# Attention scores in a hybrid encoder layer: 64 queries of two heads over 320 keys, and the softmax division moved to the output stage

## The chip, the cores and the metric

The kernel runs on one core of one Trainium2 chip. The metric is device microseconds (us) of one execution. Five engines work side by side, each through its own instructions in order: TensorE (PE in the profile, its weight loads PEld), VectorE (DVE), ScalarE (ACT), GpSimd (POOL) and SyncE (SP), which only issues transfers. They wait for one another through semaphores.

## The reference

One layer over 4096 positions of width 1024: RMS norm, one input projection, two groups of heads side by side, one output projection, residual, and a last RMS norm. Group A is a bidirectional mLSTM (4 heads of 128), group B windowed attention. The change touches group B:

```python
scores = jnp.einsum('bnqhgd,bnkhd->bnhgqk', qb, kw) * (B_HEAD_DIM ** -0.5)   # 8 query heads, 2 kv heads, 64 wide
...
mask = (jnp.abs(rel) <= WINDOW)[None, :, :] & key_ok[:, None, :]             # WINDOW = 128, BLOCK = 128
scores = jnp.where(mask[None, :, None, None], scores + bias, NEG_INF)
sink_l = sink.astype(jnp.float32).reshape(B_KV_HEADS, Q_PER_KV)[:, :, None]
m = jnp.maximum(jnp.max(scores, axis=-1), sink_l)
p = jnp.exp(scores - m[..., None])
denom = jnp.sum(p, axis=-1) + jnp.exp(sink_l - m)
out = jnp.einsum('bnhgqk,bnkhd->bnqhgd', p, vw) / denom.transpose(0, 1, 4, 2, 3)[..., None]
...
y_b = windowed_gqa(qh, kh, vh, sink, rel_bias) * jax.nn.silu(z_b.astype(jnp.float32))
y = jnp.concatenate([y_a, y_b], axis=-1).astype(x.dtype)
return x + y @ w_out.astype(x.dtype)
```

A block of 128 queries sees three blocks of 128 keys, but each query only the 257 keys within 128 of it; 64 neighbouring queries together see 64 + 256 = 320 keys.

## The kernel before, in words

All work is in float32, most products split into a high and a low part (tiles of type fp32r), so that a product is two or three matmuls. Four passes follow one another: `pass1` (norm and transposes of x, the q, k and v projections of group B and all its attention, the gates of group A, and the first values of group A), `pass2` (group A's q, k, v and its backward states), `pass3` (group A's scan, its gates, the first part of group B's gate) and `tail` (the rest of group B's gate in `zunits`, then the output projection with a Strassen scheme, two row blocks a pair, class `OutPair`).

Attention goes in 64 slots; slot `sl` is query block `n = sl // 2` and key head `kv = sl % 2`, with four query heads. In `att_a(sl, g)` head g's scores are made by two matmuls (high and low part of k) of up to 384 columns into the PSUM tile `sp`; one DVE instruction (line 280) adds the bias, writes the tile `s` in SBUF and takes the row maximum. After the fourth head: the maximum against the sink (line 286), four exponentials on ACT that also sum (line 288), the sink's own term (290, 291), the sum and its reciprocal (292, 293), and four multiplications on POOL by that reciprocal (line 295). `att_t` transposes the four heads' tiles in pieces of 128 keys on PE (line 307), `att_o` multiplies them by v (line 321), and ACT and DVE add the two halves of the result into `ab` (lines 332, 333), which goes to DRAM as `at_d`.

On PE the order is the one in which the Python code is written (`manual_schedule`): `interleave` spreads the attention pieces of `slot` between projection matmuls. On the other engines a scheduler sets the order by priority and by its own estimate of when inputs are there. Each engine then runs its list strictly in order. At the end of pass 1 the hooks `w2_load` (splitting the weights of group A's projections, lines 478 to 483) and `gate1`, `gate2`, `gate3` run between the last slots; `gp` (line 595) needs `G`, the end of a chain of DVE instructions on 128x256 (lines 566 to 577).

Keys sit in tiles `kk` of 512 columns, the first 256 copied from the tile before (line 391, DVE). The pool `w8` has 12 buffers of 8 KB a partition for weights, `kk` and bias; the pool `x4` has 14 buffers of 4 KB, which in the output stage hold a pair's two input tiles `y` and its seven operands `yo`.

In the output stage each pair is seven products of 12 matmuls; `prep(i)` makes operand i of the next pair (sums on DVE, a high part on ACT, a low part on DVE, line 1195), `evict` adds the products into the rows (line 1220), `finish` norms and stores them.

Of the kernel before, what the change touches and what calls it, by code (L numbers as in the profile page):

```python
# [36 lines left out]
def setup(nc, tc, A, es):  # L37
# [126 lines left out]
def pass1(c):  # L164
    nc, tc, A = c.nc, c.tc, c.A
    NB = 16
    with ExitStack() as es:
# [56 lines left out]
        def small_loads():  # L224
            r = {}
            r["oh"] = xtile(c, [33, 512], F32, "oh")
            nc.sync.dma_start(r["oh"], A["onehot"])
            r["rb"] = wk.tile([33, 8], F32, name="rb")
            nc.gpsimd.memset(r["rb"][32:33, :], 1.0)
            nc.sync.dma_start(r["rb"][0:32, :], A["rel_bias"])  # L230
            r["gb"] = c.cp.tile([128, 2, 2, 4], F32, name="gb")
            nc.sync.dma_start(r["gb"], A["gate_b"].partition_broadcast(128).rearrange("p (a b d) -> p a b d", a=2, b=2))
            sink = r["sink"] = c.cp.tile([128, 8], F32, name="sink")
            nc.sync.dma_start(sink, A["sink"].partition_broadcast(128))
            r["nsink"] = c.cp.tile([128, 8], F32, name="nsink")
            nc.vector.tensor_scalar(r["nsink"], sink, -1.0, None, ALU.mult)
            return [r[k] for k in ("oh", "rb", "gb", "sink", "nsink")]
# [10 lines left out]
        def bias_gather():  # L248
            bias.extend(c.wp.tile([128, 4, 384], F32, tag="w8", name=f"bias{j}") for j in range(2))
            flat = c.bv_d.rearrange("h q r -> (h q r)")  # L250
            for t in range(2):
                for a in range(4):
                    src = bass.AP(tensor=flat.tensor, offset=flat.offset + t * 4 * 32 * 512 + 127 - 32 * a,
                                  ap=[[511, 32], [32 * 512, 4], [1, 384]])
                    nc.sync.dma_start(bias[t][32 * a:32 * a + 32, :, :], src)

        KK, Q, V, XT, ST = {}, {}, {}, {}, {}

        def att_a(sl, g):
# [6 lines left out]
            qb, qc = Q[n // 2], (n % 2) * 128  # L266
            hs = slice(kv * 4, kv * 4 + 4)
            if g == 0:
# [3 lines left out]
            mx, ng, rs, sk, rd = [st[:, i, :] for i in range(5)]  # L272
            h = kv * 4 + g
            sp = c.ps("a", [128, 384], f"sp{n}_{h}")
            qt = qb[h // 2][:, h % 2, qc:qc + 128]
            for z in range(2):
                nc.tensor.matmul(sp[:, jl:jr], qt, kk[:, kv, z, col - 128 + jl:col - 128 + jr],  # L277
                                 start=(z == 0), stop=(z == 1))
            s = wk.tile([128, 384], F32, tag="s", bufs=13, name=f"s{n}_{h}")
            nc.vector.tensor_tensor_reduce(out=s[:, jl:jr], in0=sp[:, jl:jr], in1=bias[kv][:, g, jl:jr],  # L280
                                           op0=ALU.add, op1=ALU.max, scale=1.0, scalar=-3e38,
                                           accum_out=mx[:, g:g + 1])
            ps.append(s)
            if g < 3:
                return
            nc.vector.scalar_tensor_tensor(ng, mx, -1.0, nsink[:, hs], ALU.mult, ALU.min)  # L286
            for g in range(4):
                nc.scalar.activation(ps[g][:, jl:jr], ps[g][:, jl:jr], AF.Exp, bias=ng[:, g:g + 1],  # L288
                                     accum_out=rs[:, g:g + 1])
            nc.vector.tensor_add(sk, sink[:, hs], ng)  # L290
            nc.scalar.activation(sk, sk, AF.Exp)
            nc.vector.tensor_add(rd, rs, sk)
            nc.vector.reciprocal(rd, rd)
            for g in range(4):
                nc.gpsimd.tensor_tensor(out=ps[g][:, jl:jr], in0=ps[g][:, jl:jr],  # L295
                                        in1=rd[:, g:g + 1].broadcast_to([128, jr - jl]), op=ALU.mult)

# [14 lines left out]
        def att_o(sl, i):  # L312
# [16 lines left out]
            o = slice(64, 128) if kv == 0 else slice(0, 64)  # L329
            ov = op.rearrange("p (g q) -> p g q", g=4)  # L330
            with tc.high_priority(offset=EV):
                nc.scalar.copy(ab[a], ov[o])
                nc.vector.tensor_add(ab[a], ov[a], ab[a])  # L333
            if kv:
# [41 lines left out]
        def kproj(b):  # L376
            R = {}

            def unit(k, j):
# [10 lines left out]
                if b > 0:  # L390
                    nc.vector.tensor_copy(kk[:, :, :, 0:256], f32(KK[b - 1][:, :, :, 256:512]))
                with tc.high_priority(offset=EV):
# [46 lines left out]
        def qproj(b):  # L439
# [3 lines left out]
            def unit(m, k, j):  # L443
# [7 lines left out]
                if k < KT - 1 or j < 2:  # L451
                    return
                qt = wk.tile([128, 2, 256], F32R, tag="q", bufs=6, name=f"q{b}_{m}")
                with tc.high_priority(offset=EV):
                    for z in range(2):
                        a = slice(z * 64, z * 64 + 64)
                        o = slice(64 - z * 64, 128 - z * 64)
                        nc.scalar.activation(qt[a, z, :], qp[a, :], AF.Copy, scale=0.125)
                    for z in range(2):
                        a = slice(z * 64, z * 64 + 64)  # L460
                        o = slice(64 - z * 64, 128 - z * 64)
                        nc.vector.scalar_tensor_tensor(qt[o, z, :], qp[a, :], 0.125, f32(qt[a, z, :]),
                                                       ALU.mult, ALU.subtract)
# [147 lines left out]
def gate3(c, wk):  # L611
# [20 lines left out]
    nc.gpsimd.memset(one, 1.0)  # L632
    c.g = cl, cm, a, b, ml, dec, one


# [68 lines left out]
def pass2(c):  # L704
    nc, tc, A = c.nc, c.tc, c.A
    with ExitStack() as es:
# [137 lines left out]
        for b in range(7, -1, -1):  # L844
# [306 lines left out]
class OutPair:  # L1151
    def __init__(self, c, wk, j):
# [3 lines left out]
        for i in range(2):  # L1156
            n = 2 * j + i
            y = xtile(c, [128, KT, 128], F32, f"y{n}")
            nc.sync.dma_start(y, c.y_d[n])
            self.y.append(y)  # L1160
        if j == NCH // 2 - 1:
            for i in range(2):
# [100 lines left out]
def tail(c):  # L1263
    nc, tc, A = c.nc, c.tc, c.A
    c.psum({"pj": 8})
    with ExitStack() as es:
# [13 lines left out]
        for b in range(1, 8):  # L1280
# [55 lines left out]
        for j in range(NCH // 2):  # L1336
# [3 lines left out]
            for i in (0, 1, 2, 3, 5, 4, 6) if end else range(7):  # L1340
                p.product(i, None if end or i == 0 else (lambda i=i: nxt.prep(i - 1)))
                if i in ((2, 3) if end else (3, 5)) and j:
                    finish(2 * j - (1 if i == (3 if end else 5) else 2), p.dve)
# [31 lines left out]
def host(x, norm_w, w_in, conv_w, conv_b, gate_b, mhn_w, sink, rel_bias, w_out, final_norm_w):  # L1375
# [18 lines left out]
        "conv_b": a(a(conv_b)[0].reshape(8, 128).T),  # L1394
        "gate_b": a(gate_b)[0], "mhn": a(a(mhn_w)[0].reshape(4, 128).T), "sink": a(sink)[0],
        "rel_bias": a(rel_bias), "w_out": a(a(w_out)[0][rp]), "fnw": a(final_norm_w), "onehot": onehot,
# [17 lines left out]
```

## Time and profile before

| | |
|---|---|
| median of 3 runs | 2251.96 us (2250.21 to 2254.26) |
| the profiled execution | 2251.49 us, of which the span from first to last instruction is 2249.8 us |
| mean granted clock of TensorE | 0.996 |
| PE | 2200.6 us busy, 98% of the span |
| PEld | 1912.0 us, 85% |
| DVE | 1464.8 us, 65% |
| ACT | 1094.3 us, 49% |
| POOL | 628.8 us, 28% |
| bytes moved | 376.08 MB |

By place in the span: pass 1 to about 646 us, pass 2 to 1230 us, pass 3 and the gate to 1930 us, the output stage to the end. A group row of the profile has the line, engine, operation, tiles and shapes, the count, then busy time and mean ns of one, then the engine's idle time just before and what ended it. Matmuls overlap one another, so the mean ns of one is longer than the distance from one to the next; the latter is read from start times.

### The profile page before, as it was taken

To read this page: it belongs to the slowest core of one execution; us is meant where nothing else is said; L and a number is where in the kernel's file an instruction comes from. 1 tells how busy PE (TensorE), PEld (TensorE's weight loads), DVE (VectorE), ACT (ScalarE), POOL (GpSimd) and SP (SyncE) were. 2 spreads that over 40 slices of the span, in tenths; PEclk is the share of its full clock that TensorE was granted. 3 is DMA by queue.
4 is the path that set the end of the run, shared out by engine and by line. 5 is a ranking of instruction groups with operands and counts; after the bars stand their busy time and mean duration, and the time that the engine had idled before them with its cause. 6 is when DMAs were issued, how large, how long until landed. Compare 5 with 4: busy or idle time off the path is not lost.

```text
span 2249.8 us, 36150 instructions
## 1 busy us (share of the span) xinstructions
PE 2200.6 (98%) x12432; PEld 1912.0 (85%) x12432; DVE 1464.8 (65%) x3253; ACT 1094.3 (49%) x2710; POOL 628.8 (28%) x978
## 2 busy tenths in 40 slices
PE   6999999999989999999999999999999999999998
PEld 6999999999888888888888788888888888888887
DVE  5888888888966655665568555555554452766776
ACT  5777877787743433443346444444443231333332
POOL 2545454544623112211122111112111111112222
PEclk9999999999999999999999999999999999999999
DMA  8332323231224414442464877667776799466664
GB/s 236 124 106 93 121 78 127 76 123 57 94 76 152 142 62 148 160 141 70 138 208 154 290 245 237 225 211 246 237 229 191 274 364 307 143 166 169 169 170 129
DMA packets 257803, 376.08 MB, mean 167 GB/s; under 512 B 19507, under 2 KB 151219, under 8 KB 257620
## 3 DMA queue, kind: packets, MB, share of 16 engines
q1 hardware_dynamic: 238452, 307.90, 42.6%
q0 software_dynamic: 19024, 65.68, 9.7%
q8 instruction: 98, 1.61, 0.3%
q14 instruction: 85, 0.70, 0.1%
q10 hardware_dynamic: 144, 0.20, 0.0%
HBM read 253.18 MB, written 120.52 MB: 166 GB/s over the span
## 4 chain that ended last, share of the span: by engine, by line
PE 89%; DMA 4%; DVE 3%; ACT 2%; issue 1%; SPq 0%; POOL 0%; POOLq 0%; DVEq 0%; ACTq 0%
PE up L759 15%; PE o L1206 14%; PE zp L1050 7%; PE op L1050 7%; PE qp L449 7%; PE v2p L732 7%; PE op L321 4%; PE sp L277 4%; PE tp L307 3%; PE zbp L154 3%; PE zbp L156 3%; PE zbp L155 3%; PE num L1003 2%; PE num L1002 2%; PE kp L385 2%; PE vp L417 2%
## 5 line engine op out<-in xcount | busy, mean ns | idle before, releaser
L759 PE MATMUL up<-xb,w 128*128 128x512 f32 x1344 | 338.6, 396 | 0.0
L1206 PE MATMUL o<-wo,yo 128*128 128x512 f32 (+1 forms) x1356 | 312.1, 392 | 0.0
L1206 PEld LDWEIGHTS o<-wo,yo 128*128 128x128 f32 x1356 | 253.1, 188 | 59.1
L759 PEld LDWEIGHTS up<-xb,w 128*128 128x128 f32 x1344 | 243.9, 189 | 47.2
L295 POOL TENSOR_TENSOR s<-s,st 128x384 f32<-128x384 f32 (+1 forms) x256 | 205.2, 833 | 233.2 <-ACT pt L309 83.2
L777 DVE SCALAR_TENSOR_TENSOR qk<-U,cw,qk 128x512 f32<-128x512 f32 x256 | 190.2, 755 | 92.6 <-ACT qk L775 87.9
L449 PE MATMUL qp<-xT,wqb 128*128 128x256 f32 x1536 | 246.6, 289 | 0.2 <-DVE xT L362 0.2
L449 PEld LDWEIGHTS qp<-xT,wqb 128*128 128x128 f32 x1536 | 220.1, 191 | 9.5 <-issue 1.1
L1050 PE MATMUL op<-w,xs 128*128 128x512 f32 x720 | 202.4, 408 | 1.1 <-DMA xs<-xT_d 1.1
L1050 PE MATMUL zp<-w,xs 128*128 128x512 f32 x720 | 187.8, 401 | 1.8 <-DVE z L1059 1.8
L288 ACT ACTIVATE s<-s,st 128x384 f32<-128x384 f32 (+1 forms) x256 | 153.1, 600 | 28.6 <-DVE st L286 27.9
L732 PE MATMUL v2p<-w,xb 128*128 128x512 f32 x672 | 157.6, 394 | 0.8 <-DMA xb<-xT_d 0.8
L280 DVE CUSTOM_DVE_ANT_0 s<-sp,bias 128x384 f32<-128x384 f32 (+1 forms) x256 | 138.6, 542 | 27.3 <-PE sp L277 16.1
L1050 PEld LDWEIGHTS zp<-w,xs 128*128 128x128 f32 x720 | 130.7, 188 | 28.9 <-DVE z L1059 2.3
L732 PEld LDWEIGHTS v2p<-w,xb 128*128 128x128 f32 x672 | 126.0, 188 | 31.1 <-DMA xb<-xT_d 1.7
L1017 ACT ACTIVATE hs<-num,r 128x128 f32<-128x128 f32 x128 | 46.9, 368 | 215.8 <-DVE r L1014 168.5
L1050 PEld LDWEIGHTS op<-w,xs 128*128 128x128 f32 x720 | 126.5, 189 | 22.8 <-ACT hs L1017 1.5
L277 PE MATMUL sp<-kk,q 128*128 128x384 f32 (+1 forms) x512 | 134.6, 344 | 3.1 <-DVE st L280 3.1
L310 DVE TENSOR_TENSOR pt<-tp,pt 128x512 fp32r<-128x512 f32 x188 | 128.5, 684 | 13.7 <-ACT pt L309 9.8
L309 ACT CAST pt<-tp 128x512 fp32r<-128x512 f32 x188 | 109.9, 585 | 55.6 <-PE tp L307 53.1
L321 PE MATMUL op<-pt,v 128*128 128x512 f32 x376 | 121.8, 405 | 7.9 <-DVE ab L333 7.8
L307 PE MATMUL tp<-ident,s 128*128 128x128 f32 x752 | 112.8, 272 | 0.0
(259 smaller groups left out, 4456.3 us busy)
## 6 DMA issues: line engine op xcount, KB each, us to landing
xT_d<-xT SPq DMA_DIRECT2D x128, 256.0 KB, 2.3
xc<-xT_d SPq DMA_DIRECT2D x64, 512.0 KB, 8.2
xs<-xT_d SPq DMA_DIRECT2D x120, 256.0 KB, 6.5
xb<-xT_d SPq DMA_DIRECT2D x48, 514.0 KB, 9.2
x<-x SPq DMA_DIRECT2D x32, 512.0 KB, 4.8
E<-m_d SPq DMA_DIRECT2D x64, 256.0 KB, 4.8
W<-w_d SPq DMA_DIRECT2D x64, 256.0 KB, 5.9
y<-y_d SPq DMA_DIRECT2D x32, 512.0 KB, 4.1
```

Of the source, the lines that this page charges most:

```text
L277: nc.tensor.matmul(sp[:, jl:jr], qt, kk[:, kv, z, col - 128 + jl:col - 128 + jr], start=(z == 0), stop=(z == 1))
L280: nc.vector.tensor_tensor_reduce(out=s[:, jl:jr], in0=sp[:, jl:jr], in1=bias[kv][:, g, jl:jr], op0=ALU.add, op1=ALU.max, scale=1.0, scalar ...
L288: nc.scalar.activation(ps[g][:, jl:jr], ps[g][:, jl:jr], AF.Exp, bias=ng[:, g:g + 1], accum_out=rs[:, g:g + 1])
L295: nc.gpsimd.tensor_tensor(out=ps[g][:, jl:jr], in0=ps[g][:, jl:jr], in1=rd[:, g:g + 1].broadcast_to([128, jr - jl]), op=ALU.mult)
L307: nc.tensor.transpose(tp[:, g * 128:(g + 1) * 128], ps[g][:, j * 128:(j + 1) * 128], c.ident)
L321: nc.tensor.matmul(op, vt, pt[:, z, :], start=(i == 0 and z == 0), stop=(i == len(js) - 1 and z == 1))
L449: nc.tensor.matmul(qp, wq[k // 2][:, k % 2, w, m * 128:m * 128 + 128], x[k], start=(k == 0 and j == 0), stop=(k == KT - 1 and j == 2))
L732: nc.tensor.matmul(vp, a, wv[k // 2][:, k % 2, m, :], start=(k == 0 and j == 0), stop=(k == KT - 1 and j == 2))
L759: nc.tensor.matmul(up[:, 0:hi - lo], w[k // 2][:, k % 2, a, cs], x, start=(k == 0 and j == 0), stop=(k == KT - 1 and j == 2))
L777: nc.vector.scalar_tensor_tensor(acc, U[:, t:t + 512], cw[:, cm, t:t + 1], acc, ALU.mult, ALU.add)
L1050: nc.tensor.matmul(P[nm], XS[n](a, k), w[:, m, :], start=(k == 0 and j == 0), stop=(k == KT - 1 and j == 2))
L1206: nc.tensor.matmul(p, a[:, z, k, :], w[k // 2][:, k % 2, m, lo:hi], start=k == 0 and z == 1, stop=k == 3 and z == 0 and m == 0)
```

## The change

Scores: instead of one head's 128 queries over 384 keys, a piece `g` is now one half `h = g // 2` of the query block (64 queries) of two heads together (again 128 rows), over the 320 keys from 64h on. So q is stored as [4 groups of 64 queries, 2 heads, 64], the bias table is one tile [128, 4, 320] instead of two of [128, 4, 384], and the sink is loaded in the new row order. The tiles `s` become 12 fixed ones (`SB`), whose 64 columns outside the 320 are set to zero once, by POOL at the start; transposes and products with v stay as they were. In `att_o` only the column order changes.

Division: the reciprocals are kept in a tile `R`, and POOL's four multiplications are gone. After `gate4` in pass 2, `rnorm` transposes `R` on PE and stores it as `r_d`. In the output stage each `OutPair` loads the two blocks' reciprocals, each row copied to 64 partitions (tile `rb`, four transfers), and `scale` multiplies the attention half of both `y` tiles by it on DVE, before `prep(1)`.

Keys: the copy of 256 columns of `kk` goes from DVE to POOL.

```diff
+    c.r_d = dp.tile([NCH, 2, 4, 128], F32, name="r_d")
+    c.R = c.cp.tile([128, NCH, 2, 4], F32, name="R")
...
-            bias.extend(c.wp.tile([128, 4, 384], F32, tag="w8", name=f"bias{j}") for j in range(2))
+            bias.append(c.wp.tile([128, 4, 320], F32, tag="w8", name="bias"))
...
+        SB = [[wk.tile([128, 384], F32, name=f"s{h}_{i}") for i in range(6)] for h in range(2)]
+        for t in SB[0]:
+            nc.gpsimd.memset(t[:, 320:384], 0.0)
+        for t in SB[1]:
+            nc.gpsimd.memset(t[:, 0:64], 0.0)
...
+            half, m = g // 2, g % 2
+            lo, hi = max(jl, 64 * half), min(jr, 320 + 64 * half)
...
-            qt = qb[h // 2][:, h % 2, qc:qc + 128]
+            qt = qb[kv * 2 + m][:, qc // 64 + half].rearrange("p z q -> p (z q)")
             for z in range(2):
-                nc.tensor.matmul(sp[:, jl:jr], qt, kk[:, kv, z, col - 128 + jl:col - 128 + jr],
+                nc.tensor.matmul(sp[:, lo:hi], qt, kk[:, kv, z, col - 128 + lo:col - 128 + hi],
                                  start=(z == 0), stop=(z == 1))
-            s = wk.tile([128, 384], F32, tag="s", bufs=13, name=f"s{n}_{h}")
+            s = SB[half][(2 * sl + m) % 6]
...
-            nc.vector.reciprocal(rd, rd)
-            for g in range(4):
-                nc.gpsimd.tensor_tensor(out=ps[g][:, jl:jr], in0=ps[g][:, jl:jr],
-                                        in1=rd[:, g:g + 1].broadcast_to([128, jr - jl]), op=ALU.mult)
+            nc.vector.reciprocal(c.R[:, n, kv, :], rd)
...
-                    nc.vector.tensor_copy(kk[:, :, :, 0:256], f32(KK[b - 1][:, :, :, 256:512]))
+                    nc.gpsimd.tensor_copy(kk[:, :, :, 0:256], f32(KK[b - 1][:, :, :, 256:512]))
...
-                        nc.scalar.activation(qt[a, z, :], qp[a, :], AF.Copy, scale=0.125)
+                        nc.scalar.activation(qt[a, :, z, :], qv[a], AF.Copy, scale=0.125)
...
+def rnorm(c):
+    nc = c.nc
+    tp = c.ps("b", [128, 2, 128], "rtp")
+    for i in range(2):
+        nc.tensor.transpose(tp[:, i, :], c.R[:, 16 * i:16 * i + 16].rearrange("p n a g -> p (n a g)"), c.ident)
+    rt = xtile(c, [128, 2, 128], F32, "rt")
+    nc.scalar.copy(rt, tp)
+    for i in range(2):
+        nc.sync.dma_start(c.r_d[16 * i:16 * i + 16].rearrange("n a g q -> (n a g) q"), rt[:, i, :])
...
                 if b == 7 and m == 6:
                     gate4(c)
+                    rnorm(c)
...
+        self.rb = rb = xtile(c, [128, 2, 2, 4, 64], F32, f"rb{j}")
+        for i in range(2):
+            for a in range(2):
+                src = c.r_d[2 * j + i, a].rearrange("g q -> (g q)")
+                nc.sync.dma_start(rb[64 * a:64 * a + 64, i].rearrange("p h g q -> p (h g q)"), src.partition_broadcast(64))
...
+    def scale(self):
+        for i in range(2):
+            b = self.y[i][:, 4:8].rearrange("p g (h q) -> p h g q", h=2)
+            self.c.nc.vector.tensor_mul(b, b, self.rb[:, i])
...
                 p.product(i, None if end or i == 0 else (lambda i=i: nxt.prep(i - 1)))
+                if i == 0 and not end:
+                    nxt.scale()
```

PE's list is the same row by row except for the 192 or 320 columns of the `sp` matmuls and the two transposes of `R`. Three places on the other engines follow.

POOL at the end of pass 1, where `w2s` and `w2_..` are pieces of group A's weights and `s29_0` is head 0's tile of query block 29. Before:

```order
L295 TENSOR_TENSOR s29_0_8158<-s29_0_8158,st58_8154 128x384
L295 TENSOR_TENSOR s29_1_8174<-s29_1_8174,st58_8154 128x384
L295 TENSOR_TENSOR s29_2_8200<-s29_2_8200,st58_8154 128x384
L295 TENSOR_TENSOR s29_3_8235<-s29_3_8235,st58_8154 128x384
L478 TENSOR_TENSOR w2s10_8827<-w2s10_8827,nw_86 128x512
L480 TENSOR_TENSOR w2_10_8826<-w2s10_8827,w2_10_8826 128x512
L495 MEMSET v2t31_8453 128x8
```

and now, around the same weight pieces:

```order
L492 TENSOR_TENSOR w2_04_7679<-w2s04_7680,w2_04_7679 128x512
L490 TENSOR_TENSOR w2s10_8337<-w2s10_8337,nw_87 128x512
L492 TENSOR_TENSOR w2_10_8336<-w2s10_8337,w2_10_8336 128x512
L507 MEMSET v2t31_7992 128x8
L490 TENSOR_TENSOR w2s14_8356<-w2s14_8356,nw_87 128x512
L492 TENSOR_TENSOR w2_14_8355<-w2s14_8356,w2_14_8355 128x512
```

The multiplications between the weight pieces are gone.

DVE at the end of pass 1, around the instruction that completes `G` (line 577 before, 589 now). Before:

```order
L310 TENSOR_TENSOR pt61_1_8740<-tp61_1_8735,pt61_1_8740 128x512
L293 RECIPROCAL st62_8604<-st62_8604 128x4
L333 TENSOR_TENSOR ab30_8747<-op60_8698,ab30_8747 64x512
L575 SCALAR_TENSOR_TENSOR g0_8581<-g0_8581 128x256
L280 ISA s31_7_8755,st63_8690<-sp31_7_8752,bias1_326 128x256
L280 ISA st63_8690 128x1
L483 SCALAR_TENSOR_TENSOR w2_22_8946<-w2s22_8947,nw_86,w2_22_8946 128x512
L483 SCALAR_TENSOR_TENSOR w2_22_8946<-w2s23_8951,nw_86,w2_22_8946 128x512
L577 SCALAR_TENSOR_TENSOR G_89<-g0_8581 128x256
```

and now:

```order
L306 RECIPROCAL R_91<-st62_8130 128x4
L320 TENSOR_TENSOR pt61_0_8236<-tp61_0_8231,pt61_0_8236 128x512
L587 SCALAR_TENSOR_TENSOR g0_8107<-g0_8107 128x256
L320 TENSOR_TENSOR pt61_1_8255<-tp61_1_8250,pt61_1_8255 128x512
L589 SCALAR_TENSOR_TENSOR G_90<-g0_8107 128x256
L292 ISA s1_1_156,st63_8208<-sp63_3_8267,bias_352 128x192
L292 ISA st63_8208 128x1
L344 TENSOR_TENSOR ab30_8262<-op60_8215,ab30_8262 64x2x4x64
```

`G` is now completed ahead of the last scores, the addition into `ab30` and the two weight pieces.

DVE in the output stage, while pair 4's products run; `y12`, `y13` are the inputs of pair 6, `xr8` the rows of pair 4. Before:

```order
L1220 TENSOR_TENSOR xr8_21117<-o2_4_0_21150,xr8_21117 128x512
L1183 TENSOR_TENSOR s6_1_21306<-y13_21196 128x512
L1195 TENSOR_TENSOR yo5_5_21251<-s5_4_21223,yo5_5_21251 128x512
L1195 TENSOR_TENSOR yo5_6_21261<-y11_21047,yo5_6_21261 128x512
L1184 TENSOR_TENSOR s6_1_21306<-s6_1_21306,y12_21194 128x512
```

and now:

```order
L1254 TENSOR_TENSOR xr8_20674<-o2_4_0_20709,xr8_20674 128x512
L1229 TENSOR_TENSOR yo5_5_20815<-s5_4_20787,yo5_5_20815 128x512
L1207 TENSOR_TENSOR y12_20753<-y12_20753,rb6_20757 128x2x4x64
L1207 TENSOR_TENSOR y13_20755<-y13_20755,rb6_20757 128x2x4x64
L1254 TENSOR_TENSOR xr8_20674<-o3_4_0_20729,u4_20673 128x512
```

The two multiplications by `rb6` stand ahead of the eviction of pair 4's product 3.

More of the change, by code (lines that the diff above doesn't have):

```diff
@@ L232, in small_loads @@
             nc.sync.dma_start(r["gb"], A["gate_b"].partition_broadcast(128).rearrange("p (a b d) -> p a b d", a=2, b=2))
-            sink = r["sink"] = c.cp.tile([128, 8], F32, name="sink")
-            nc.sync.dma_start(sink, A["sink"].partition_broadcast(128))
-            r["nsink"] = c.cp.tile([128, 8], F32, name="nsink")
+            sink = r["sink"] = c.cp.tile([128, 2, 2, 2], F32, name="sink")
+            for z in range(2):
+                nc.sync.dma_start(sink[64 * z:64 * z + 64].rearrange("p a h m -> p (a h m)"),
+                                  A["sink"][z].partition_broadcast(64))
+            r["nsink"] = c.cp.tile([128, 2, 2, 2], F32, name="nsink")
             nc.vector.tensor_scalar(r["nsink"], sink, -1.0, None, ALU.mult)
@@ L461, in unit @@
                         o = slice(64 - z * 64, 128 - z * 64)
[L462 removed]
+                        nc.vector.scalar_tensor_tensor(qt[o, :, z, :], qv[a], 0.125, f32(qt[a, :, z, :]),
                                                        ALU.mult, ALU.subtract)
```

39 lines of the change are left out of this document (22 added, 17 removed).

## The prediction

> **What bounds the kernel now.** I read the page first: what is busy, and the chain that ended last.
>
> ```profile
> span 2249.8 us, 36150 instructions
> PE 2200.6 (98%) x12432; PEld 1912.0 (85%) x12432; DVE 1464.8 (65%) x3253; ACT 1094.3 (49%) x2710; POOL 628.8 (28%) x978
> PE 89%; DMA 4%; DVE 3%; ACT 2%; issue 1%; SPq 0%; POOL 0%; POOLq 0%; DVEq 0%; ACTq 0%
> ```
>
> PE is 89% of the chain. A busy PE could still be a PE that waits inside, so the next view is the busy time by stretches: the steady part of pass 1, its end, and the output stage (columns: length, then busy us and instructions of PE, PEld, DVE, ACT, POOL, then clock, DMA share, GB/s).
>
> ```profile
> 120.00:560.00 440.00, 438.78 (x3274) 423.27 (x3273) 375.67 (x1044) 346.48 (x913) 229.26 (x323) 1.00 0.29 99
> 560.00:640.00 80.00, 68.98 (x414) 60.66 (x413) 69.24 (x173) 57.77 (x146) 44.30 (x56) 0.96 0.31 96
> 2000.00:2100.00 100.00, 100.00 (x432) 80.87 (x432) 70.87 (x115) 34.73 (x64) 22.00 (x30) 1.00 0.59 158
> ```
>
> In pass 1 PE is full although DVE has 85%; from 560 to 640 us PE falls to 86% and DVE is as busy as PE; in the output stage PE is full with DVE at 71%. What PE waited for between 555 and 700 us, then at the start of the program, by the view of waits:
>
> ```profile
> PE op L321 <- DVE ab L333: 6.7, 5, 2.5
> PE gp L595 <- DVE G L577: 4.4, 1, 4.4
> ...
> PE sp L277 <- DVE st L280: 2.9, 1, 2.9
> DVE s L280 <- DMA bias<-bv_d: 5.7, 1, 5.7
> ```
>
> So a saved column on PE in pass 1 is saved time, one for one, except at the end of that pass, where DVE holds PE for 6.7 + 4.4 = 11.1 us.
>
> **The sum. Score matmuls.** Their price is the distance between starts, not the mean duration. PE in order of time, at a place where matmuls of three widths alternate:
>
> ```profile
> 605.72 0.52 PE L277 MATMUL sp<-kk,q 128*128 128x384 f32 x2
> 606.07 0.63 PE L498 MATMUL v2p<-w,xT 128*128 128x512 f32 x2
> 606.54 0.60 PE L307 MATMUL tp<-ident,s 128*128 128x128 f32 x4
> ...
> 607.67 0.40 PE L277 MATMUL sp<-kk,q 128*128 128x256 f32 x2
> 607.91 0.63 PE L498 MATMUL v2p<-w,xT 128*128 128x512 f32 x2
> ```
>
> Two of 384 columns take 606.07 - 605.72 = 0.35 us, two of 512 take 0.47, two of 256 take 0.24: a straight line, (0.47 - 0.24) / 4 = 0.0575 us for 64 columns of a pair. Nothing here shows 320 columns. It can't cost more than 384 (gain 0) nor, I take it, less than 256 (gain 0.11 a pair, 26 us in all); on a line through three points I take the middle. How many there are:
>
> ```profile
> L277 PE MATMUL sp<-kk,q 128*128 128x384 f32 x480 | 127.4, 346 | 0.2 <-DVE st L280 0.2
> L280 DVE CUSTOM_DVE_ANT_0 s<-sp,bias 128x384 f32<-128x384 f32 x240 | 132.1, 551 | 20.1 <-PE sp L277 14.8 <-POOL G L434 2.0 <-POOL s L295 0.3
> L280 DVE CUSTOM_DVE_ANT_0 s<-sp,bias 128x256 f32<-128x256 f32 x16 | 6.5, 416 | 7.2 <-DMA bias<-bv_d 5.7 <-PE sp L277 1.3
> L288 ACT ACTIVATE s<-s,st 128x384 f32<-128x384 f32 x240 | 145.2, 607 | 23.5 <-DVE st L286 22.8
> L295 POOL TENSOR_TENSOR s<-s,st 128x384 f32<-128x384 f32 x240 | 193.2, 836 | 223.4 <-ACT pt L309 83.2 <-PE sp L277 66.3 <-DVE st L293 42.2
> L391 DVE CAST kk<-kk 128x1024 fp32r<-128x1024 f32 x15 | 11.5, 765 | 0.0
> L208 POOL TENSOR_TENSOR x<-x,rstd 128x1024 f32<-128x1024 f32 x30 | 56.3, 1898 | 1.2
> ```
>
> 240 pairs x 0.0575 = 13.8 us; of the 16 pairs at the ends of the sequence eight shrink from 256 to 192 columns, 0 to 0.5 us, 0.2 taken. Together 14.0 us, all on the path.
>
> The Trainium skill would have it smaller: "TensorE: Matmul & The Clock Gate", section "Back-to-back issue gap", gives a sustained 81 ns a matmul at 128 columns and 131 at 512, by which I estimate 8.3 ns for 64 columns and 4.1 us for 496 matmuls. The trace differs: 432 matmuls of 512 columns in 100 us are 231 ns each, and the measurement decides.
>
> **DVE, ACT and POOL in pass 1.** Line 280 costs (551 - 416) / 128 = 1.05 ns a column, so 67 ns less on 240, 16 us less on DVE; the exponentials on ACT shrink likewise. The key copies leave DVE (11.5 us) and POOL loses 193 us plus the 16 short ones. Before 560 us none of this is on the path, since PE does not wait there. The transposes come one POOL step of four times 0.84 us earlier, which nothing waits for. DVE gains more than its own instructions: it stands behind POOL. The maximum's instruction on four columns, beside the POOL instruction that runs at that time, and the whole group of its neighbour:
>
> ```profile
> 577.38 1.52 POOL L480 TENSOR_TENSOR w<-w2s,w 128x512 fp32r<-128x512 f32 x1 [0.73 <-ACT w L479]
> 577.68 1.24 DVE L286 SCALAR_TENSOR_TENSOR st<-st,nsink 128x4 f32<-128x4 f32 x1
> L290 DVE TENSOR_TENSOR st<-sink,st x64: 145/162/1434, 52.4 to 629.6; 128x4 f32<-128x4 f32 x64
> L290 DVE TENSOR_TENSOR st<-sink,st 128x4 f32<-128x4 f32 x64 | 23.5, 366 | 0.6
> ```
>
> A thing of some 160 ns took 1.24 us and ended with POOL's instruction (578.90); line 290 averages 366 ns against a median of 162. With four POOL multiplications a slot gone, most of that goes.
>
> **The end of pass 1.** `gp`'s wait ends with a chain that now stands earlier in DVE's list:
>
> ```profile
> 629.01 1.20 PE L595 MATMUL gp<-tri,G 128*128 128x128 f32 x4 [4.37 <-DVE G L577]
> ...
> 626.08 2.03 DVE L483 SCALAR_TENSOR_TENSOR w<-w2s,nw,w 128x512 fp32r<-128x512 f32 x2
> 628.04 0.82 DVE L577 SCALAR_TENSOR_TENSOR G<-g 128x256 f32<-128x256 f32 x1
> ```
>
> Two weight pieces (2.0 us), an `ab` and a score addition (about 1.1) now follow `G`: of 4.4 us some 4 go. The five waits for `ab` sum to 6.7 us. Over the two slots or so between them DVE gets 8 x 0.067 = 0.5 us shorter and is held up less behind POOL, 0 to 1.1 us by the example, while PE arrives 8 x 0.0575 = 0.46 us sooner; so each shrinks by 0 to 1.2, and I take 2 us of the 6.7. Together 6 us; the ends are 11 (all gone) and -2 (DVE no faster, PE waits out its own gain five times). What is late next there is the additions into `ab`.
>
> **What is added.** The key copy on POOL: between DVE's 0.77 and the 1.90 of a POOL multiplication of the same size, nearest to the latter; 15 x 1.9 = 28 us if uncovered, or less than nothing on DVE. Cover: it reads keys made one block earlier, POOL sheds seven times as much, and behind it stand only short additions to `G`. I take 0. The q tiles and `ab` are written in runs of 64: same element counts, 0, covered by DVE's spare 15%.
>
> The start: twelve POOL memsets and the bias.
>
> ```profile
> 0.81 0.20 POOL masks.py:197 MEMSET ident<- 128x128 f32 x1 [0.29 <-POOLq L1404]
> 5.70 0.56 POOL L191 TENSOR_TENSOR rstd_first<-rstd_first,nhalf 128x1 f32<-128x1 f32 x1 [3.96 <-DVE rstd_first L190]
> ```
>
> Twelve at 0.20 or less are 2.4 us inside POOL's 3.96 us of idleness: 0. Four bias transfers instead of eight, each a sixth narrower, on SP's queue ahead of the first score addition: of PE's 2.9 us there 0 to 2.9 go, 0.5 taken. The sink's second transfer stands with loads that nobody waits for.
>
> `rnorm`: two transposes on PE, half of the row of four above, which spans 0.60 us, so 0.3 us, plus a wait for the PSUM buffer that `mp` leaves:
>
> ```profile
> 664.84 0.67 PE L644 MATMUL dp<-ml,rows 1*128 1x256 f32 x2
> 665.01 0.16 DVE L647 COPY cl<-mp 128x4 f32<-128x4 f32 x1 [0.88 <-PE mp L641]
> ```
>
> The buffer is free at 665.17, before `dp` is through, so the wait adds nothing: 0.3 us in all. Its ACT copy and two stores on SP have over a thousand us before anyone needs them.
>
> The output stage: 32 multiplications on DVE and 64 transfers on SP.
>
> ```profile
> L1183 DVE TENSOR_TENSOR s<-y 128x512 f32<-128x512 f32 x16 | 10.9, 684 | 0.6 <-DMA y<-y_d 0.6
> y<-y_d SPq DMA_DIRECT2D x32, 512.0 KB, 4.1
> E<-m_d SPq DMA_DIRECT2D x64, 256.0 KB, 4.8
> 42.51 3.68 SPq L255 DMA_DIRECT2D bias<-bv_d  x8
> ```
>
> A pair is 84 matmuls, 19.4 us. DVE works 70.87% of it, 13.8 us, and two multiplications of 0.684 us make 15.2: 4.2 us stay free. PE has the next pair's operands before it begins, so 1.4 us on DVE costs 0. If that cover went, 14 pairs x 1.4 = 19 us would. The `rb` transfers queue on SP behind `y` only, and behind them `y` of the next pair; at the stage's start the late weights stand behind `rb` too.
>
> Sum against the profiled execution: 2251.5 - 14.0 - 6.0 - 0.5 + 0.3 = 2231.3 us; the median of the runs is 0.5 above that execution, so 2232 us.
>
> **Rivals.** (1) The waits at the end of pass 1 stay, DVE being reordered without arriving sooner: 2252 - 14.2 = 2238. For it: PE arrives sooner too; against it: POOL's hold-ups and the order of `G`. (2) All waits of PE named above go, at the start too: 14 + 11.1 + 2.9 less 0.3, 2224. For it: POOL is nearly empty. (3) A matmul's spacing goes in steps, and 320 cost what 384 do: 2252 - 6.2 = 2246. Against it: 256, 384 and 512 lie on a line. The skill's gap rule is the nearest relative of this one. (4) The other side: `rb` lands late. DVE's multiplication of pair j + 2 stands ahead of pair j's eviction of product 3. If `rb` gets its buffer only as DVE comes to it, four issues of 3.68 / 8 = 0.46 us and a landing of 4.8 make DVE stand 6.6 us, 2.4 more than it has free; 14 pairs x 2.4 = 34 us, 2266. It decides slower from 4.2 + 20 / 14 = 5.6 us a pair. For it: the 14 buffers now serve ten tiles a pair, not nine; against it: `y`, loaded by the same queue, made DVE wait 0.6 us in the whole stage, and `rb` is given back as soon as it is used. (5) The key copy comes late for the scores: up to 2232 + 28 = 2260.
>
> **How the numbers follow.** The forecast has 0.58, (1) 0.21, (2) 0.07, (3) 0.04, (4) 0.07, (5) 0.03. Changes of 0.2% (4.5 us) are about what can be told from none. The forecast's own range is 2227 to 2236 (4 to 5 us of its end-of-pass term either way); with (1) and (2) it becomes 2224 to 2240, and a little for the spacing of 320 columns on the upper side: 2225 to 2242. Faster: the forecast, (1), (2) and most of (3), 0.89; same: the rest of (3) and mild forms of (4) and (5), 0.04; slower 0.07.
>
> **What would show it.** Right: two score matmuls of 320 columns start 0.29 to 0.30 us apart from the next; POOL in pass 1 falls by about 200 us; line 290's mean falls towards 0.16 us; PE's wait for `G` is under 1 us; pass 2 begins 20 us sooner, at about 626; pass 2, pass 3 and the output stage last as long as before; PE has no idle time in the output stage, and the multiplications by `rb` take 0.68 us each. Wrong: a wait of DVE for `rb` of over 4 us a pair, PE waiting for `yo`, `sp` waiting for the copy of `kk`, or new waits for `ab`.

## The result, and the profile after

The changed kernel takes 2231.2 us, median of three runs, against 2251.8 us; the ratio is 0.9905, 95% interval 0.9885 to 0.9924. A fourth run, left out here, took 8614.8 us at a mean granted clock of 0.238, against 0.995 to 0.997 in the three. The forecast was 2232. The profiled execution took 2229.31 us with a span of 2227.6, so 22.2 us less than the profiled execution before; the medians differ by 20.6. The page after, first the span and engines, then the chain that ended last:

```profile
span 2227.6 us, 35563 instructions
PE 2183.8 (98%) x12434; PEld 1895.8 (85%) x12434; DVE 1455.9 (65%) x3270; ACT 1077.7 (48%) x2711; POOL 429.9 (19%) x749
PE 74%; DMA 11%; issue 5%; DVE 5%; ACT 3%; POOL 1%; SPq 0%; POOLq 0%; DVEq 0%; ACTq 0%
```

POOL lost 199 us, DVE only 9. The chain now runs for 11% through transfers: followed back from the end, it goes pair by pair through the one that adds the residual (`xr<-x`), the norm and the store, no longer through PE, although PE is full there all the same. The three stretches again; the work of pass 1 now comes 16 to 24 us earlier, so the second reaches beyond the pass, and the row of 545 to 620 us is nearer to the same work. Then what PE waited for at the end of pass 1:

```profile
120.00:560.00 440.00, 439.32 (x3363) 424.01 (x3361) 368.85 (x1061) 345.29 (x943) 84.60 (x155) 1.00 0.30 100
560.00:640.00 80.00, 73.34 (x469) 64.06 (x469) 61.32 (x151) 49.40 (x122) 13.06 (x26) 1.00 0.29 90
545.00:620.00 75.00, 68.25 (x427) 58.91 (x426) 63.75 (x171) 55.00 (x140) 17.09 (x27) 1.00 0.31 96
2000.00:2100.00 100.00, 100.00 (x432) 80.74 (x431) 75.89 (x124) 33.14 (x62) 21.93 (x30) 1.00 0.69 185
...
PE op L331 <- DVE ab L344: 5.7, 5, 2.1
PE tp L317 <- DVE pt L320: 0.9, 1, 0.9
```

PE is as full as before in the steady part, with 89 more matmuls recorded in the same 440 us. The wait for `G` is gone, those for `ab` are not, and one for `pt` is new. At the end of the pass PE is busy 91% of the time instead of 86%, and the clock, 0.96 from 560 to 640 us before, is 1.00.

Two profiles of one kernel differ by place, so a second one of each was taken (experiments e5_again and e12_before). PE's list is the same in both kernels, so the start of the same matmul can be compared; the table is worked out from those starts, with the places named by the time in the kernel before:

| place | first profiles | second profiles |
|---|---|---|
| 60 us, first attention | -2.3 | +0.3 |
| 560 us, steady part done | -16.4 | -12.7 |
| 646 us, pass 1 done | -24.4 | -21.2 |
| 1746 us, pass 3 | -24.7 | -21.2 |
| PE's last matmuls | -24.1 | -20.6 |
| end of the span | -22.2 | -18.8 |

Everything is won in pass 1, 8 us of it in its last 86 us, and 1.9 us are given back after PE has finished.

### The profile page after: what moved, and what is told of

It reads as the page before. It is cut to its first block, busy times and chain, and to the rows that moved or that the text cites. A ratio compares the mean times of both kernels' runs of the same rounds, so it can differ in the third digit from the quotient of the medians.

```text
span 2227.6 us, 35563 instructions
## 1 busy us (share of the span) xinstructions
PE 2183.8 (98%) x12434; PEld 1895.8 (85%) x12434; DVE 1455.9 (65%) x3270; ACT 1077.7 (48%) x2711; POOL 429.9 (19%) x749
## 4 chain that ended last, share of the span: by engine, by line
PE 74%; DMA 11%; issue 5%; DVE 5%; ACT 3%; POOL 1%; SPq 0%; POOLq 0%; DVEq 0%; ACTq 0%
PE up L782 15%; PE zp L1074 7%; PE op L1074 7%; PE v2p L755 7%; PE qp L460 6%; DMA xr<-x 5%; PE op L331 3%; PE tp L317 3%; PE zbp L156 3%; PE zbp L158 3%; PE zbp L157 3%; PE sp L289 3%; PE num L1027 2%; PE num L1026 2%; PE kp L396 2%
## 5 line engine op out<-in xcount | busy, mean ns | idle before, releaser
L301 ACT ACTIVATE s<-s,st 128x320 f32<-128x320 f32 (+1 forms) x256 | 139.8, 548 | 29.3 <-DVE st L299 28.9
L292 DVE CUSTOM_DVE_ANT_0 s<-sp,bias 128x320 f32<-128x320 f32 (+1 forms) x256 | 122.0, 477 | 25.5 <-PE sp L289 19.6
L289 PE MATMUL sp<-kk,q 128*128 128x320 f32 (+2 forms) x512 | 119.8, 315 | 1.4 <-DVE st L292 1.4
L995 ACT ACTIVATE E<-E,TM 128x128 f32<-128x128 f32 x256 | 81.0, 389 | 42.7 <-POOL E L992 42.5
```

What stands on the lines that cost most here:

```text
L289: nc.tensor.matmul(sp[:, lo:hi], qt, kk[:, kv, z, col - 128 + lo:col - 128 + hi], start=(z == 0), stop=(z == 1))
L292: nc.vector.tensor_tensor_reduce(out=s[:, lo:hi], in0=sp[:, lo:hi], in1=bias[0][:, kv * 2 + m, lo - 64 * half:hi - 64 * half], op0=ALU.add ...
L301: nc.scalar.activation(ps[g][:, kept(g)], ps[g][:, kept(g)], AF.Exp, bias=ng[:, g:g + 1], accum_out=rs[:, g:g + 1])
```

## The experiments

**e1_wide: the columns alone.**

```diff
-                nc.tensor.matmul(sp[:, lo:hi], qt, kk[:, kv, z, col - 128 + lo:col - 128 + hi],
+                nc.tensor.matmul(sp[:, jl:jr], qt, kk[:, kv, z, col - 128 + jl:col - 128 + jr],
```

> The changed kernel, but the score matmuls compute all 384 columns again (the 64 that nobody reads are left unused); bias addition, exponentials and everything else stay at 320. Theory (the width is paid on PE, one for one): 480 matmuls go from 0.148 to 0.1755 us apart, so 13.2 us come back; part of it may be taken out of the waits for ab at the end of pass 1 (5.7 us in the changed kernel), since PE arrives later there: 2240 to 2245 us, and the stretch of 440 us in the steady part shows PE full as before. Rival (the gain came from a lighter DVE, ACT and POOL, and the columns were not on the path): 2234 us or less.

2246.6 us, ratio 0.9983 (0.9974 to 0.9992). By place it is 13.1 us behind the changed kernel's first profile at 590 us, as 480 x 27.5 ns says. Against five profiles with the same score matmuls, the 390 of them in the steady part make 10.7 to 11.6 us, so 13.2 to 14.3 for all 480. At the end of pass 1, 1.5 us are taken out of the waits. Another 4 us appear behind pass 1, which the edit does not touch, and put the time 1.6 us above the expected range. The theory holds, the rival falls. The spacing itself, in the changed kernel's PE in order of time:

```profile
577.00 0.46 PE L289 MATMUL sp<-kk,q 128*128 128x320 f32 x2
577.29 0.40 PE L510 MATMUL v2p<-w,xT 128*128 128x512 f32 x1
...
581.42 0.45 PE L289 MATMUL sp<-kk,q 128*128 128x320 f32 x2
581.71 0.39 PE L510 MATMUL v2p<-w,xT 128*128 128x512 f32 x1
```

Two matmuls of 320 columns take 0.29 us: on the line through 256, 384 and 512, no step.

**e2_poolnorm and e4_before_nonorm: POOL's multiplications against the order of `G`.** The first puts them back into the changed kernel, where `G` stands early in DVE's list; the second takes them out of the kernel before, where it stands late.

```diff
             nc.vector.reciprocal(c.R[:, n, kv, :], rd)
+            for g in range(4):
+                nc.gpsimd.tensor_tensor(out=ps[g][:, kept(g)], in0=ps[g][:, kept(g)],
+                                        in1=c.R[:, n, kv, g:g + 1].broadcast_to(...), op=ALU.mult)
...
-                    rnorm(c)
...
-        self.rb = rb = xtile(...)        # and its four transfers, and both calls of scale()
```

> The changed kernel with the division where it was: POOL multiplies the four tiles of a slot by the reciprocals, the output stage has neither rb transfers nor the multiplications of y, and R is not transposed. G stays at its new, early place in DVE's list. Theory 1 (at the end of pass 1 it was the order of DVE's list that cost PE 4.4 us): PE waits less than 1 us for G, and the time is that of the changed kernel less what the end of the program loses now (1.9 us) and the transposes (0.3): 2229 to 2231 us. Theory 2 (it was POOL's multiplications holding DVE up): the waits for G and ab come back, 4 to 7 us more at the end of pass 1, 2233 to 2236 us.

```diff
-            for g in range(4):
-                nc.gpsimd.tensor_tensor(out=ps[g][:, jl:jr], in0=ps[g][:, jl:jr],
-                                        in1=rd[:, g:g + 1].broadcast_to([128, jr - jl]), op=ALU.mult)
```

> The kernel before without POOL's four multiplications a slot (so the probabilities stay undivided); nothing else changed, and G keeps its old, late place in DVE's list, behind two weight pieces. Theory 1 (order): PE still waits 2.5 us or more for G, the waits for ab shrink a little, 2249 to 2251 us. Theory 2 (POOL holds DVE up): the wait for G falls below 1 us and those for ab to half, 5 to 8 us less, 2244 to 2247 us. By both, PE's time between 120 and 560 us stays as it is, and the instructions on four columns take 0.16 us where POOL's multiplications held them up.

e2_poolnorm took 2230.8 us (0.9911, 0.9895 to 0.9926), e4_before_nonorm 2242.5 (0.9968, 0.9956 to 0.9981). What PE waited for at the end of pass 1, in e4_before_nonorm, then in e2_poolnorm:

```profile
PE op L318 <- DVE ab L330: 4.9, 4, 1.6
PE gp L592 <- DVE G L574: 3.1, 1, 3.1
```

```profile
PE op L334 <- DVE ab L347: 7.5, 5, 4.2
PE tp L320 <- DVE st L303: 0.5, 1, 0.5
PE tp L320 <- DVE pt L323: 0.3, 1, 0.3
```

Both theories have half. Without the multiplications but with the old order, 3.1 of the 4.4 us for `G` stay; with the new order that wait is gone even where POOL multiplies. But with the multiplications one wait for `ab` grows to 4.2 us. The place, POOL's and DVE's rows of e2_poolnorm:

```profile
595.90 3.43 POOL L308 TENSOR_TENSOR s<-s,R 128x320 f32<-128x320 f32 x4
...
596.11 1.05 DVE L498 SCALAR_TENSOR_TENSOR w<-w2s,nw,w 128x512 fp32r<-128x512 f32 x1 [1.23 <-ACT w L497]
597.09 0.94 DVE L586 TENSOR_TENSOR g<-g 128x256 f32<-128x256 f32 x1
597.94 0.81 DVE L591 TENSOR_SCALAR g<-G 128x256 f32<-128x256 f32 x1
```

Inside POOL's 3.43 us three DVE instructions take 2.80 us that take 1.4 in the changed kernel (0.75, 0.41 and 0.28), and the addition into `ab` stands behind them; ahead of them DVE waited 1.23 us for ACT. PE's waits at the end of pass 1 are 11.1 us with late `G` and multiplications, 8.0 without the multiplications, 8.3 with early `G` and multiplications, 6.6 with neither. By place e2_poolnorm loses 4.0 us on the changed kernel between 560 and 646 us, as the second theory said: 1.7 us of waits and 2.5 us of slow matmuls behind the wait of 4.2 us (such matmuls are shown further down). Its time lies in the first theory's range all the same, with an end of the program of 7.4 us after PE's last matmul instead of 9.1. So of the 8 us at the end of pass 1 the order, with the narrower scores, keeps about 4 and a POOL without multiplications alone 4.7. e4_before_nonorm gained more than either theory gave it: those 4.7 us, the rest at the start (2.1 us before 120 us) and behind pass 1, of the size by which two profiles of one kernel differ there; I leave that rest open.

**e3_noscale, e8_lastx and e6_scalepool: the end of the program.** e3_noscale leaves out `rb` and `scale`; e8_lastx gives the last pair row tiles of its own; e6_scalepool multiplies on POOL.

```diff
-        self.rb = rb = xtile(...)        # e3: and its four transfers
-                nxt.scale()              # e3: both calls
...
-            c.XR[n] = wk.tile([128, D], F32, tag="x", bufs=4, name=f"xr{n}")
+            c.XR[n] = xtile(c, [128, D], F32, f"xr{n}")        # e8: in the last pair only
...
-            self.c.nc.vector.tensor_mul(b, b, self.rb[:, i])
+            self.c.nc.gpsimd.tensor_mul(b, b, self.rb[:, i])   # e6
```

> The changed kernel without the 64 rb transfers and the 32 multiplications of y in the output stage, so the attention half of y stays undivided. Theory 1 (the multiplications are hidden except at the very end, where DVE is 2.2 us further behind PE than before): from PE's last matmul to the end of the span 7.2 us as in the kernel before instead of 9.1, and 1.9 us less in all, 2229.3 us. Theory 2 (the end is late for another reason, and 32 multiplications of 0.68 us cost nothing): no change, 2231 us.

> The changed kernel with the last pair's two row tiles in the pool x4, which is no longer full there, instead of the pool of four tiles x; nothing else. Theory 1 (the 1.9 us at the end are a wait for a row buffer: DVE's lag of 2.7 us makes the store of the pair before late, and the last pair's rows wait for that store): from PE's last matmul to the end of the span 7.2 to 7.6 us instead of 9.1, DVE waits for no store there, and 1.5 to 1.9 us less in all. Theory 2 (DVE is simply behind by that much at the end): 9.1 us as before, no change.

> The changed kernel with the two multiplications of y a pair on POOL instead of DVE (about 1.14 us each by the weight pieces of the same size). Theory 1 (DVE is relieved by 1.4 us a pair, and the end of the program gets back its 1.9 us): 7.2 us from PE's last matmul to the end, 2229.3 us. Theory 2 (the instructions of DVE with two inputs in SBUF stand behind POOL's 2.3 us a pair, which is more than the 1.4 us saved): DVE's sums and low parts, 0.69 us each now, get longer where they meet POOL, and the end stays at 9 us or grows; 2231 to 2233 us.

The same places in the kernel before and in the changed one: PE's last 32 matmuls, and DVE where it adds the residual to the last pair's rows.

```profile
2230.08 0.69 DVE L1229 TENSOR_TENSOR xr<-u,xl 128x512 f32<-128x512 f32 x1
...
2237.80 4.76 PE L1206 MATMUL o<-wo,yo 128*128 128x512 f32 x32
```

```profile
2208.39 0.69 DVE L1263 TENSOR_TENSOR xr<-u,xl 128x512 f32<-128x512 f32 x1 [1.82 <-DMA out<-xr]
...
2213.66 4.84 PE L1240 MATMUL o<-wo,yo 128*128 128x512 f32 x32
```

Before, PE ends at 2242.56 and the span at 2249.8, 7.2 us later; after, at 2218.50 and 2227.6, 9.1 us later. Against the start of that row DVE is 2.4 us later (5.27 us ahead of it instead of 7.72), and it waited for a store. Without `rb` and `scale` the end takes 7.2 us again (2229.1 us, 0.9903, 0.9890 to 0.9917); e6_scalepool keeps the transfers and has the early end too, so the 1.9 us are the price of the multiplications on DVE. With row tiles of its own DVE waits for no store, but the end takes 8.4 us (2231.7 us, 0.9910, 0.9897 to 0.9924): the buffer is a third of it, the rest is DVE's lag itself, and that run's time shows no gain. On POOL the end takes 7.1 us (2228.4, 0.9895, 0.9881 to 0.9909), although DVE is hardly relieved: 142.3 us busy in ten pairs after 144.0. The groups of DVE in the output stage, first of the changed kernel, then of e6_scalepool:

```profile
L1229 DVE TENSOR_TENSOR yo<-s,yo 128x512 fp32r<-128x512 f32 x53 | 35.5, 688 | 47.4 <-ACT yo L1228 47.3
L1207 DVE TENSOR_TENSOR y<-y,rb 128x512 f32<-128x512 f32 x26 | 16.8, 685 | 2.6 <-DMA rb<-r_d 2.6
```

```profile
L1229 DVE TENSOR_TENSOR yo<-s,yo 128x512 fp32r<-128x512 f32 x54 | 43.9, 832 | 49.4 <-ACT yo L1228 49.4
L1207 POOL TENSOR_TENSOR y<-y,rb 128x512 f32<-128x512 f32 x26 | 34.5, 1326 | 52.2 <-DMA rb<-r_d 46.1 <-PE o L1240 6.1
```

The low parts, two inputs in SBUF, grow from 688 to 832 ns, as the second theory said, and POOL's multiplication takes 1326 ns where 1.14 us had been expected; DVE is 7.68 us ahead of PE's last 32 matmuls again. That the end is early nevertheless I put down to DVE's list, in which no multiplication stands ahead of an eviction; no run tells this apart.

**e9_scale6: how much DVE time was free.** The two multiplications are done six times a pair.

```diff
-                    nxt.scale()
+                    for _ in range(6):
+                        nxt.scale()
```

> The changed kernel with the two multiplications of y by rb repeated, six times each a pair instead of once (so the attention half of y is divided too often). Theory 1 (free time on DVE counts from start to start, 0.60 us an instruction, and with 143.98 us busy in ten pairs of 194 us some 5.0 us a pair are free): ten more instructions are 6.0 us, 1.0 more than free, 14 pairs: 14 us, about 2245 us. Theory 2 (the reckoning of the prediction, 0.684 us each and 4.2 us free without any): 8.2 us against 4.2, 4.0 too many, 56 us, 2287 us. Theory 3 (DVE's idle time is waiting for ACT and can't be used): up to 84 us, 2315 us.

2269.7 us, ratio 1.0077 (1.0062 to 1.0092): 38.5 us more than the changed kernel, between the theories. PE's waits in the output stage, and a stretch of it by windows:

```profile
PE o L1240 <- DVE yo L1229: 24.6, 13, 3.2
...
2006.00:2218.00 212.00, 193.78 (x785) 153.24 (x784) 197.38 (x321) 59.35 (x111) 46.21 (x56) 0.95 0.61 165
```

PE stood 24.6 us in 13 waits, on the mean 1.8 us in each of 14 pairs. Ten more instructions are 6.0 us from start to start, so 4.2 us of the 5.0 left to DVE by its busy time could be used. Most of the other 14 us is the clock, 0.95 on the mean of these 212 us: PE runs slowly after such waits (below). The end of the program does not grow with the multiplications: it takes 8.8 us after PE's last matmul, where PE had been waiting for DVE pair by pair.

**e10_kkdve: the key copies on DVE again.**

```diff
-                    nc.gpsimd.tensor_copy(kk[:, :, :, 0:256], f32(KK[b - 1][:, :, :, 256:512]))
+                    nc.vector.tensor_copy(kk[:, :, :, 0:256], f32(KK[b - 1][:, :, :, 256:512]))
```

> The changed kernel with the key copies on DVE again (15 of 0.77 us) instead of POOL (15 of 1.04 us). Theory 1 (hidden on either engine, since PE waits for neither in the steady part): PE's time from 120 to 560 us as in the changed kernel within 0.5 us, total 2230 to 2232 us. Theory 2 (it relieves DVE where PE waits): up to 3 us longer, at the end of pass 1.

2230.9 us (0.9906, 0.9890 to 0.9923). From 120 to 560 us it gains 0.7 us on the changed kernel's profile, from 560 to the end of pass 1 it loses 0.1: the copy costs nothing on either engine.

**e5_again and e12_before: the scatter by place.** No edit.

> The changed kernel once more, on the chip on which the next three run, to see how far two profiles of one kernel differ by place. If the gain of 2.3 us before the first 60 us of the span, which kernels with the new bias table showed only in part, is scatter of the first transfers, that place moves by 1 us or more against the first profile; if it belongs to the change, it stays within 0.3. From PE's last matmul to the end 9.1 us either way. Time 2229 to 2232 us.

> The kernel before once more, to see how far two of its profiles differ by place. If the 2.3 us before the first 60 us of the span are scatter, its PE reaches the projections of the second block, at 60.0 us in the first profile, 1 us or more earlier or later; the waits at the end of pass 1 (6.7 and 4.4 us) and the 7.2 us after PE's last matmul stay within 0.5 us.

2230.7 us (0.9906, 0.9891 to 0.9920), and 2251.4 us in one run. At 60 us the changed kernel's second profile is 1.9 us later than its first; the second of the kernel before is 0.8 us earlier at 60 us and 1.9 at 120. So the start is scatter. The end repeats: 9.0 us after PE's last matmul in the changed kernel, 7.2 in the kernel before; the waits at the end of pass 1 of the kernel before are 7.3 and 4.4 us, one 0.1 outside what I expected.

**e7_w2pool and e11_best: a better version.** e7_w2pool moves six of DVE's weight pieces to POOL; e11_best adds a second buffer for `ab` to e6_scalepool.

```diff
-                if k % 4 == 0:
+                if k % 2 == 0:                                        # e7
...
-                AB[n] = wk.tile([128, 4, 128], F32, tag="ab", bufs=1, name=f"ab{n}")
+                AB[n] = wk.tile(...) if n % 2 else bias[1]            # e11: bias[1] lies behind the bias table in its tile
```

> The changed kernel with twice as many pieces of group A's weights split on POOL (every second one instead of every fourth: 12 of 24), six of DVE's 18 pieces of 0.75 us moved to POOL at 1.14 + 1.38 us each. Theory 1 (at the end of pass 1 DVE's load is what PE still waits for, and POOL is empty now): the waits for ab and pt fall from 6.6 us to 2 to 4, and 2 to 4 us less in all, 2227 to 2229 us. Theory 2 (POOL's longer instructions hold DVE up and deliver late): PE waits as long or longer, now also for the weight pieces or for G, which has moved back in DVE's list; 2231 to 2236 us.

> The changed kernel with two things added: the multiplications of y on POOL, and a second buffer for ab (every second query block's ab lies in the unused part of the bias tile). Theory 1 (at the end of pass 1 the additions into ab are late partly because the one ab tile is still being stored, 0.8 us of ACT's waiting in the changed kernel; the end of the program gets its 1.9 us back): 1 to 2 us less than with the multiplications on POOL alone (2228.4), 2226 to 2228 us, PE's waits for ab under 5 us. Theory 2 (the waits for ab are DVE's and ACT's, held by the weight pieces and their transfers): the second buffer changes nothing, 2228 to 2229 us.

e7_w2pool: 2229.7 us (0.9898, 0.9883 to 0.9913), not to be told from the changed kernel by its time; by place it loses 2.8 us at the end of pass 1, where PE now waits 2.5 us at `gp`, so what shows is the second theory. e11_best: 2226.4 us (0.9887, 0.9872 to 0.9902), the lowest median of all, though its interval overlaps that of the changed kernel. Its waits for `ab` are 3.7 us, after 5.7 in the changed kernel but 4.3 in e6_scalepool with its one buffer, and by place its pass 1 ends 0.2 us later than that of e6_scalepool. Its gain over the changed kernel at the end of the program (7.1 us after PE's last matmul) is shown; that of the second buffer is not.

## Why the prediction was right

**The columns.** 14.0 us predicted, 13.2 by the spacing, and 13.1 came back in e1_wide (13.2 to 14.3 by the steady part). Rival (3), a step in the spacing, is out.

**The end of pass 1.** 6.0 us predicted, of which 4 for `G` and 2 for `ab`. `G` gave all its 4.4, by the order of DVE's list: POOL's absence alone took 1.3 of them. For `ab` and the new wait for `pt` together 6.6 us remain of 6.7, so that term failed: DVE was not held up less. The step behind it, "most of that goes", was wrong. The four-column instructions, in the kernel before and in the changed one (L286, L290, L292 are now L299, L303, L305):

```profile
L286 DVE SCALAR_TENSOR_TENSOR st<-st,nsink 128x4 f32<-128x4 f32 x64 | 12.4, 194 | 1.4
L292 DVE TENSOR_TENSOR st<-st 128x4 f32<-128x4 f32 x64 | 12.6, 196 | 20.9 <-ACT st L291 20.5
```

```profile
L299 DVE SCALAR_TENSOR_TENSOR st<-st,nsink 128x4 f32<-128x4 f32 x64 | 24.9, 389 | 1.4
L303 DVE TENSOR_TENSOR st<-sink,st 128x4 f32<-128x4 f32 x64 | 10.4, 163 | 1.0
L305 DVE TENSOR_TENSOR st<-st 128x4 f32<-128x4 f32 x64 | 18.6, 291 | 3.3 <-ACT st L304 2.4
L402 POOL CAST kk<-kk 128x1024 fp32r<-128x1024 f32 x15 | 15.6, 1040 | 250.6 <-DVE kk L413 235.1 <-ACT s L301 15.5
```

Line 290's successor fell to 163 ns as predicted, but its neighbours rose, and the three together went from 48.5 to 53.9 us. The traces show why. Of the 20 instructions of these groups that took over 0.25 us in the kernel before, 14 fell in POOL's multiplication of `x` in the norm (line 208), 12 of them on line 290; only one fell in the multiplications of line 295, to which the prediction put them down. In the new order L299 meets the multiplication of `x`, 12 times too, and 14 of L305 fall in the key copy, which the change itself put on POOL; with that copy on DVE L305 is short again. POOL's row of line 208 and the DVE row inside it in the kernel before, a like pair in the changed one, then L305 in e10_kkdve:

```profile
323.98 3.76 POOL L208 TENSOR_TENSOR x<-x,rstd 128x1024 f32<-128x1024 f32 x2
324.76 1.14 DVE L290 TENSOR_TENSOR st<-sink,st 128x4 f32<-128x4 f32 x1
...
577.82 1.85 POOL L492 TENSOR_TENSOR w<-w2s,w 128x512 fp32r<-128x512 f32 x1 [0.79 <-ACT w L491]
578.44 1.25 DVE L299 SCALAR_TENSOR_TENSOR st<-st,nsink 128x4 f32<-128x4 f32 x1
...
L305 DVE TENSOR_TENSOR st<-st 128x4 f32<-128x4 f32 x64 | 10.7, 167 | 3.0 <-ACT st L304 2.4
```

The sum came out because something else went that was not in it, the slow matmuls behind the long waits. In the kernel before, behind the 2.46 us wait:

```profile
588.13 1.22 PE L321 MATMUL op<-pt,v 128*128 128x512 f32 x2 [2.46 <-DVE ab L333]
589.15 1.05 PE L449 MATMUL qp<-xT,wqb 128*128 128x256 f32 x4
590.00 0.84 PE L277 MATMUL sp<-kk,q 128*128 128x384 f32 x2
590.64 0.80 PE L449 MATMUL qp<-xT,wqb 128*128 128x256 f32 x3
591.27 0.60 PE L307 MATMUL tp<-ident,s 128*128 128x128 f32 x4
...
585.00:590.00 5.00, 2.54 (x11) 2.15 (x11) 4.92 (x12) 1.51 (x4) 1.77 (x2) 0.78 0.36 105
```

From 588.13 to 591.27 are 3.14 us; at the usual spacing (0.232, 0.119 and 0.1755 us for 512, 256 and 384 columns) these eleven matmuls take 1.65. So 1.5 us more; by the same reckoning 1.6 us behind the wait for `G`. In the changed kernel's two profiles neither is left: behind the first one's longest wait, 2.1 us, the two matmuls of `op` take 0.73 us. 4.5 us of waits and 3.1 us of clock are 7.6 us; by place the stretch became 7.9 and 8.5 us shorter, some of it by the narrower scores. How this splits is partly chance. In e6_scalepool, whose pass 1 has the same code, the same wait is followed by slow matmuls, and the next one shrinks from 1.85 to 0.17 us:

```profile
611.50 1.22 PE L331 MATMUL op<-pt,v 128*128 128x512 f32 x2 [2.27 <-DVE ab L344]
...
617.78 0.72 PE L331 MATMUL op<-pt,v 128*128 128x512 f32 x2 [0.17 <-DVE ab L344]
```

The stretch from 560 to 646 us of the kernel before takes 78.0 us in that run and 78.1 in the changed kernel.

**The start.** 0.5 predicted, nothing that can be told from scatter measured.

**The key copy, `rnorm`, the `rb` transfers.** 0 to 0.3 us predicted and found; DVE waited 2.6 us for `rb` in 26 multiplications, where rival (4) needed 5.6 a pair. Rival (5) is out by e10_kkdve.

**The multiplications of `y`.** "1.4 us on DVE costs 0" held for PE, which waits nowhere in the output stage, but not for the end: cover lasts as long as PE has work, and 1.9 us stood behind its last matmul. As prices, 4.2 us free and 0.684 us each were about right for the wrong reason: an instruction costs 0.60 us from start to start, and of DVE's idle time a part is waiting for ACT.

**The sum.** 13.2 + 4.5 + 3.1 - 1.9 = 18.9 us against 20.2 predicted, and the medians' 20.6; the second pair of profiles has 18.8. Two errors, 3.1 us left out and 1.9 us not charged, nearly cancelled with the `ab` term: the number came out better than its working by luck.

## What to carry to other kernels

When PE is full, count saved columns from start to start, and look for the rest at the seams: the ends of the stages, where another engine holds PE. Work that is hidden beside PE comes out where PE stops, so ask of each hidden instruction what it leaves late at the last matmul. Before charging held-up DVE instructions to one group on POOL, look at which POOL rows they fall in: here it was mostly another group, and which instruction meets which is set by the order.

## What the hardware showed

A wait of PE can cost more than its length. At the end of pass 1, after all eight gaps of 2.65 us or more from one matmul's start to the next's in these runs, the following matmuls ran at 1.8 to 2 times their spacing for 3 to 5 us; between 2.3 and 2.65 us this happened after three gaps of eight. The length alone does not decide it: in the output stage of e9_scale6 a gap of 2.92 us passed without, while gaps of 2.23 and 2.28 us were followed by seven or eight matmuls 0.427 us apart instead of 0.232. In e9_scale6, 24.6 us of waiting cost 38.5. The Trainium skill, "TensorE: Matmul & The Clock Gate", section "HAM oscillation — how this bites in real kernels", has gaps above about 3.4 us as the ones to avoid; the trace shows the drop behind a wait of 2.46 us, so here the measurement is the stricter one.

While a POOL instruction runs, a DVE instruction with its inputs in SBUF can be held until it ends: the 12 of L299 that met the multiplication of `x` took 1.25 to 1.26 us for four columns and ended 0.02 us behind POOL's instruction. The 14 of line 292, with one input in PSUM, that met the same multiplications were not held: all together took 0.1 us more than their medians. The page "GPSIMD Engine Reference", section "1. Specifications", of the Trainium skill has the two engines share their SBUF interfaces, for DVE instructions with two SBUF inputs or in a two-port mode; these runs agree. Whether POOL is held in turn they do not show: in e6_scalepool 24 of its 32 multiplications of `y` took 1.28 to 1.32 us, like five of the six weight pieces of line 492, and eight 1.42 to 1.75.
